# The last pass of a SwiGLU down projection: one bank at a time, and two kinds of additions on GpSimd

## The chip, the cores and the metric

One core of a Trainium2 chip. The metric is the device time of one execution in microseconds (us), lower is better. The kernel's output is compared with a float32 reference. Engines are named as in the profile: PE (TensorE, with its weight loads PEld), DVE (VectorE), ACT (ScalarE), POOL (GpSimd) and SP (SyncE, which here only issues DMAs).

## The reference

One decoder layer on 512 tokens of width 2048: a mixer of 16 attention heads with an output projection and a residual, then a SwiGLU block with a residual. All of it is float32. The change lies in the SwiGLU block, in its last product:

```python
def _swiglu(h, w_gate, w_up, w_down):
    return (jax.nn.silu(h @ w_gate) * (h @ w_up)) @ w_down

# D_MODEL = 2048, SEQ = 512, D_FF = 5632
x = x + _hybrid_mixer(_rms_norm(x, attn_norm[l]), ...)
h = _rms_norm(x, ffn_norm[l])
x = x + _swiglu(h, w_gate[l], w_up[l], w_down[l])
```

## The kernel before

**Arithmetic.** Every float32 operand of a matmul is split into a high part and the rest ("split": ACT copies the operand into the rounded format, DVE subtracts the copy from the operand). A product is then three matmuls: high by high, high by rest, rest by high. In the code `w[0]`, `w[1]` are the two parts of a weight, `a[0]`, `a[1]` those of the activations. All DVE work of two operands goes through the helper `tt` (L77), all ACT copies through `act` (L80), so these two lines stand for many steps, and the tiles' names tell them apart.

**Block products.** The gate, up and down products are cut into 2 by 2 blocks, and the blocks are multiplied by schemes that need seven products in place of eight, with sums of weights and of activations made beforehand and sums of results made afterwards. Time up to about 1684 us is the mixer and the gate and up products; the change does not touch them.

**Down product.** It runs from about 1684 us to 2120 us, in four passes (`ps_` = 0 to 3, here pass 1 to pass 4). Passes 1 and 2 make one half of the output rows, passes 3 and 4 the other. The first pass of each pair (1 and 3) does four of the seven products, the second (2 and 4, `second` true in the code) does the other three. A pass goes over 22 steps j of the inner dimension; a step with its matmuls is called a *block* here, counted from 0. Output columns of the weight are in four *quarters* q of 128, each with its own two banks of PSUM, `b[q][0]` and `b[q][1]`. A block of a second pass is 4 quarters x 3 products x 3 matmuls = 36 matmuls of 256 columns. The three products are listed in `DOWN2` (activation part, weight part, bank, half of the bank): the first goes to bank 1, the other two fill the two halves of bank 0.

**What comes before a block.** `got(j)` fetches ahead (`load_a`, `load_w`, DMAs issued by SP) and calls `splits(i)`. In a second pass `splits` first makes the sum of the freshly loaded weight `r[:, :T]` and a sum `t` that was kept from the pass before (`keep_t2`; in the profile `wd<-wd,t2m` or `wd<-wd,rawm`, 512 columns). This is "the sum with kept halves". Then come three splits, each a copy by ACT and a difference by DVE: the activations (768 columns, `rawm`), the kept sum `t` (512, `t2m` or `rawm`), and the pair of `r` (1024, `wd`), which needs the sum. The last block of pass 4 splits its activations last. The split weights lie in four places in turn (`WAT`), the split activations in three (`AAT`), the raw weights in three (`RING`). A block's activations can thus be copied when PE has finished the block three before it.

**Order.** From the end of the mixer on, the instructions of DVE, ACT, POOL and SP are pinned: each of these engines issues in the order in which the code makes them (`pin`, `fetch2`). The matmuls are not pinned; the compiler may move them among each other. Each of the engines waits only in its own queue.

**The last blocks of a pass** (one block, in pass 4 three together: `tail`) run quarter by quarter, and behind each quarter its results are taken from PSUM by `end(q)`, which is `last(q)`:

- passes 1 and 3: `keep1` puts the two banks into the kept tiles `cb` and `ca`. Behind pass 3, `fold_early` is left to be done during pass 4, one step per block (`next(pending, None)` after `got`): for each quarter a difference of 512 columns, one of 256, then twice a product with `rstd` on DVE and an accumulating DMA from `x1d` issued by POOL (L1019). These are 16 steps, in blocks 0 to 15 of pass 4. They are called the *fold*.
- pass 2: `finish_late`, whose rest is done during pass 3.
- pass 4: `finish(q)`: t4 = bank 1 x rstd; `ca` - t4 (the stored difference), which leaves as `out[n + 1]`; half of `cb` + t4; t62 = bank 0 x rstd; `cb` + t62, which leaves as `out[n]`. DVE does all five, SP issues the two DMAs. In the profile both t4 and t62 are `t<-pd,rstd`.

Of the kernel before, what the change touches and what calls it, by code (L numbers as in the profile page):

```python
# [12 lines left out]
OP = mybir.AluOpType  # L13
# [4 lines left out]
P = 128  # L18
D = 2048
T = 512  # L20
# [6 lines left out]
NJ = NF // 2  # L27
# [41 lines left out]
def hybrid_layer(ctx: ExitStack, tc: tile.TileContext, xT, vec, ffb, wfg, wfirst, win, cmpw, wout, wgu, wdn, out):  # L69
    nc = tc.nc  # L70
    pinned = [False]

    def pin(ins):
        return tc.keep_in_program_order(ins) if pinned[0] else ins

    def tt(*args, op):
        return pin(nc.vector.tensor_tensor(*args, op=op))  # L77
# [21 lines left out]
    def big(i):  # L99
        at = i * 2 * T + OFF_BIG[i]  # L100
        return bigm[:, at:at + 2 * T].rearrange("p (s t) -> p s t", s=2)
# [23 lines left out]
    def ftile(name):  # L125
        return pers.tile([P, T], F32, tag="f", name=name, bufs=4)
# [12 lines left out]
    def load_w(src, name):  # L139
        n = src.shape[-1]  # L140
        st = wpl.tile([P, HALF * P], F32, tag="ws", name=f"ws_{name}", bufs=3)
        load(st[:, :n], src)
        wp = wpl.tile([P, 2, HALF * P], FR, tag="wp", name=f"wp_{name}", bufs=2)
        split(wp[:, :, :n], st[:, :n])
        return wp
# [22 lines left out]
    def run(steps):  # L168
        for _ in steps:
            pass  # L170
# [86 lines left out]
    for g in range(2):  # L257
        t = ap_.tile([P, NB, 64], F32, name=f"pc{g}")
# [21 lines left out]
    live = {}  # L280
# [275 lines left out]
    def chain(*gens):  # L556
        for g in gens:
            yield from g
# [12 lines left out]
    for k in range(NK):  # L571
        xs = oxp.tile([P, T], F32, tag="ox", name=f"x_{k}", bufs=16)
        nc.sync.dma_start(xs, xT[k])
        ws = oxp.tile([P, T], F32, tag="ox", name=f"w0_{k}", bufs=16)
        nc.sync.dma_start(ws, wfirst[k])
        t = big(k)
# [13 lines left out]
        for hl in range(2):  # L590
            nc.tensor.matmul(first[4][:64], wf[:, k], t[:, hl], start=(k == 0 and hl == 0),
                             stop=(k == NK - 1 and hl == 1))
# [48 lines left out]
    h = NH - 1  # L641
# [18 lines left out]
    for i, h in enumerate(order[:-1]):  # L660
        t = big(i)
# [3 lines left out]
    t = big(NK - 1)  # L665
# [10 lines left out]
    def cut(m, at, n):  # L676
        return m[:, at:at + n]
# [117 lines left out]
    def halves(x):  # L795
        return x.rearrange("p (h t) -> p h t", h=2)

    def both(x):
        return x[:, None].to_broadcast([P, 2, 256])
# [55 lines left out]
    def fetch2(dst, src):  # L855
        d = nc.sync.dma_start(dst, src)
        tc.keep_in_program_order(d)
        return d

    def t2(j):  # L860

        m, at = (live["fa"], j - 8) if 8 <= j < 16 else (live["fy"], j if j < 8 else j - 8)
        return cut(m, at * T, T)

    def pass_of(i):
        return i // (2 * NJ), i // NJ % 2, i % NJ
# [20 lines left out]
    def load_a(i):  # L887
        second, j = pass_of(i)[1:]
        at = (8 + 2 * (turn[1] % 3)) * T
        turn[1] += 1  # L890
        rawa[i] = cut(live["fa"], at, (3 if second else 4) * 256)
        d = fetch2(rawa[i], ad[j][:, 4:7] if second else ad[j][:, 0:4])
        if i == 2:
            tc.add_manual_dep(d.ins, live["w0"].ins.name, PACE)

    def split2(dst, src):
        h = act(dst[0], src, AF.Copy)
        tt(dst[1], src, dst[0].bitcast(F32), op=OP.subtract)
        return h

    def keep_t2(i):
        r = raww.pop(i)
        tt(t2(i % NJ), r[:, T:2 * T], r[:, 2 * T:3 * T], op=OP.add)

    def splits(i):
        second, j = pass_of(i)[1:]
        n = 3 if second else 4
        m, at = WAT[i % 4]
        w = [cut(m, at + h * (4 * T + (SHIFT if i % 24 == 0 else 0)), n * T) for h in range(2)]
        m, at = AAT[i % 3]  # L910
        a = [cut(m, at + h * 4 * 256, n * 256) for h in range(2)]
        if second:
            r, t = raww.pop(i), t2(j)
            tt(r[:, T:2 * T], r[:, :T], t, op=OP.add)
        if i < 4 * NJ - 1:
            split2(a, rawa.pop(i))
        if second:
            split2([x[:, 2 * T:] for x in w], t)
            split2([x[:, :2 * T] for x in w], r[:, :2 * T])
        else:  # L920
            live.setdefault("w0", split2(w, raww[i]))
        if i == 4 * NJ - 1:
            split2(a, rawa.pop(i))
        return [[x.rearrange("p (f c) -> p f c", f=n) for x in y] for y in (w, a)]
# [19 lines left out]
    for j in range(NJ):  # L944
        for which in range(2):
            q = [ps.tile([P, T], F32, tag=tag, name=f"q{which}{j}_{i}", bufs=BUFS[tag])
                 for i, tag in enumerate(SETS[which])]
            for g in range(NG):
# [14 lines left out]
                w = split_w.pop(i)  # L963

                for wp in range(2):
                    for kk in range(2):
                        k = 2 * (ORDER[i] % NG) + kk
                        a = forms[k]
                        cs = slice(kk * P, (kk + 1) * P)
                        for fa, fb, b, h in PROD:  # L970
                            o = q[b][:, h * 256:(h + 1) * 256]
                            for xp in range(2 - wp):
                                nc.tensor.matmul(o, w[wp][:, fb, cs], a[:, xp, fa],  # L973
                                                 start=(k == 0 and h == 0 and wp == 0 and xp == 0),
                                                 stop=(g == NG - 1 and kk == 1 and wp == 1), skip_group_check=True)
# [24 lines left out]
    def banks(name, tags):  # L1000
        return [ps.tile([P, T], F32, tag=tag, name=f"{name}_{i}", bufs=BUFS[tag]) for i, tag in enumerate(tags)]
# [51 lines left out]
    def finish(q, b):  # L1053

        y = [k[:, q] for k in kept]
        n = 8 + 2 * q
        t4, t62 = ftile(f"t4_{q}"), ftile(f"t62_{q}")
        tt(halves(t4), both(b[1][:, :256]), halves(rstd), op=OP.mult)
        tt(y[1], y[1], t4, op=OP.subtract)
        fetch2(out[n + 1], y[1])  # L1060
        tt(y[0][:, :256], y[0][:, :256], t4[:, :256], op=OP.add)
        tt(t62, b[0], rstd, op=OP.mult)
        tt(y[0], y[0], t62, op=OP.add)
        fetch2(out[n], y[0])

    TAGS = ("ss", "to", "gg", "mt")
    for ps_ in range(4):
        p, second = ps_ // 2, ps_ % 2
        b = [banks(f"pd{ps_}{i}", t) for i, t in enumerate(TAGS)]
        prods = DOWN2 if second else DOWN1  # L1070
        ends = []
        extra = chain(load_w(2 * NJ), load_w(2 * NJ + 1)) if ps_ == 1 else iter(())

        def got(j):
            i = ps_ * NJ + j
            if i not in ahead:
                load_a(i)
                run(load_w(i))
                ahead[i] = splits(i)
                if not second:  # L1080
                    keep_t2(i)
            return j, *ahead.pop(i)

        def block(js, parts, end=None):
            ws = [got(j) for j in js]
            if end and ps_ < 3:

                run(extra)
                nxt = [(ps_ + 1) * NJ + n for n in range(2)]
                for i in nxt:  # L1090
                    load_a(i)
                    run(load_w(i) if i not in raww else ())
                for i in nxt:
                    ahead[i] = splits(i)
                    if ps_ == 1:
                        keep_t2(i)
            if ps_ == 0 and js[0] == 0:
                for _ in range(3):
                    next(pending)
                for i in range(2):  # L1100
                    keep_t2(i)
            next(pending, None)
            for qs in parts:
                for j, w, a in ws:
                    for q in qs:
                        for fa, fb, k, h in prods:
                            for xp in range(2):
                                nc.tensor.matmul(b[q][k][:, h * 256:(h + 1) * 256], w[0][:, fb, q * P:(q + 1) * P], a[xp][:, fa],  # L1108
                                                 start=(j == 0 and h == 0 and xp == 0), stop=False, skip_group_check=True)
                for q in qs:  # L1110
                    for fa, fb, k, h in prods:
                        for j, w, a in ws:
                            nc.tensor.matmul(b[q][k][:, h * 256:(h + 1) * 256], w[1][:, fb, q * P:(q + 1) * P], a[0][:, fa],  # L1113
                                             start=False, stop=(j == NJ - 1), skip_group_check=True)
                    if end:
                        end(q)

        def last(q):
            if not second:
                keep1(q, b[q])  # L1120
                if p:
                    ends.append(fold_early(q))
            elif p:
                finish(q, b[q])
            else:
                ends.append(finish_late(q, b[q]))
                next(ends[-1])

        each = [(q,) for q in range(4)]
        head, tail = 2 if ps_ == 0 else 1, 3 if ps_ == 3 else 1  # L1130
        block(tuple(range(head)), [range(2), range(2, 4)] if ps_ == 0 else each)
        for j in range(head, NJ - tail):
            block((j,), [range(4)])
            if j >= 16:
                next(extra, None)
        run(pending)
        block(tuple(range(NJ - tail, NJ)), each, last)
        pending = chain(*ends)

# [69 lines left out]
```

## Time and profile before

| | |
|---|---|
| median of 3 runs | 2127.51 us (2127.18 to 2128.12) |
| the profiled execution | 2128.19 us, its span 2126.4 us |
| PE | 2114.6 us busy (99%) |
| DVE | 1693.4 us busy (80%) |
| ACT | 995.5 us busy (47%) |
| POOL | 185.2 us busy (9%) |
| DMA | 349.56 MB, mean 164 GB/s |

The span is the time from the first to the last instruction that the profile has; the time of the execution contains some 1.8 us more around it. Times in the rows of a timeline are microseconds from the start of the span; a row has start, duration, engine, line, operation, the tiles written and read, the shape, the count of merged instructions and in brackets the idle time before it with what ended it. A row that merges several instructions shows their start and their whole stretch. Ends of matmuls are modelled.

### The profile page before, as it was taken

To read this page: it belongs to the slowest core of one execution; us is meant where nothing else is said; L and a number is where in the kernel's file an instruction comes from. 1 tells how busy PE (TensorE), PEld (TensorE's weight loads), DVE (VectorE), ACT (ScalarE), POOL (GpSimd) and SP (SyncE) were. 2 spreads that over 40 slices of the span, in tenths; PEclk is the share of its full clock that TensorE was granted. 3 is DMA by queue.
4 is the path that set the end of the run, shared out by engine and by line. 5 is a ranking of instruction groups with operands and counts; after the bars stand their busy time and mean duration, and the time that the engine had idled before them with its cause. 6 is when DMAs were issued, how large, how long until landed. Compare 5 with 4: busy or idle time off the path is not lost.

```text
span 2126.4 us, 36981 instructions
## 1 busy us (share of the span) xinstructions
PE 2114.6 (99%) x15137; PEld 1957.9 (92%) x15137; DVE 1693.4 (80%) x2488; ACT 995.5 (47%) x1226; POOL 185.2 (9%) x283
## 2 busy tenths in 40 slices
PE   9999999999999999999999999999999999999998
PEld 7888887888888888999999999999999999999998
DVE  6678568555657444999999999999999987889998
ACT  5455455444446333544334444343443455565553
POOL 0000000111101000111111111111111000000000
PEclk9999999999999999999999999999999999999999
DMA  5421211222222443567776777777777798479864
GB/s 194 158 73 35 67 60 45 83 86 87 87 85 65 158 143 125 162 194 211 183 198 187 185 202 187 198 190 183 205 185 199 226 337 266 150 235 330 291 180 138
DMA packets 113482, 349.56 MB, mean 164 GB/s; under 512 B 13592, under 2 KB 13592, under 8 KB 113312
## 3 DMA queue, kind: packets, MB, share of 16 engines
q1 hardware_dynamic: 85552, 270.33, 38.5%
q0 software_dynamic: 22144, 52.44, 13.6%
q10 hardware_dynamic: 5616, 24.43, 2.9%
q8 instruction: 118, 1.93, 0.4%
q14 instruction: 52, 0.43, 0.1%
HBM read 318.56 MB, written 74.73 MB: 185 GB/s over the span
## 4 chain that ended last, share of the span: by engine, by line
PE 95%; DVE 3%; ACT 1%; issue 0%; DMA 0%; ACTq 0%; DVEq 0%
PE q L973 39%; PE pd L1108 13%; PE pd L1113 6%; PE po L150 2%; PE po L148 2%; PE po L149 2%; PE ps_kf L148 1%; PE ps_kf L150 1%; PE ps_kf L149 1%; PE ps_qf L148 1%; PE ps_vf L148 1%; PE ps_qf L150 1%; PE ps_qf L149 1%; PE ps_vf L150 1%; PE ps_vf L149 1%; PE ps_qn L149 1%
## 5 line engine op out<-in xcount | busy, mean ns | idle before, releaser
L80 ACT ACTIVATE bigm<-r 128x1792 fp32r<-128x1792 f32 x174 | 298.1, 1713 | 463.0 <-PE q L973 267.7
L77 DVE TENSOR_TENSOR bigm<-r,bigm 128x1792 fp32r<-128x1792 f32 x174 | 351.5, 2020 | 14.2 <-ACT bigm L80 13.4
L77 DVE TENSOR_TENSOR r<-r 128x512 f32<-128x512 f32 x522 | 267.2, 512 | 26.3 <-DMA r<-wgu 14.2
L973 PE MATMUL q<-bigm 128*128 128x256 f32 x1848 | 217.5, 277 | 0.3
L973 PE MATMUL q<-forma,bigm 128*128 128x256 f32 x1848 | 217.0, 277 | 0.0
L973 PE MATMUL q<-formx,bigm 128*128 128x256 f32 x1848 | 217.0, 277 | 0.0
L973 PE MATMUL q<-formy,bigm 128*128 128x256 f32 x1848 | 216.8, 277 | 0.0
L973 PEld LDWEIGHTS q<-bigm 128*128 128x128 f32 x1848 | 213.2, 188 | 0.7 <-ACT bigm L80 0.3
L973 PEld LDWEIGHTS q<-forma,bigm 128*128 128x128 f32 x1848 | 213.2, 188 | 0.1
L973 PEld LDWEIGHTS q<-formx,bigm 128*128 128x128 f32 x1848 | 213.1, 188 | 0.0
L973 PEld LDWEIGHTS q<-formy,bigm 128*128 128x128 f32 x1848 | 212.9, 188 | 0.1
L122 POOL DMA_DIRECT2D wsum<-wdn x176 | 119.8, 687 | 881.2 <-ACT bigm L80 776.9
L1108 PE MATMUL pd<-bigm 128*128 128x256 f32 x1224 | 148.0, 277 | 0.0
L1108 PEld LDWEIGHTS pd<-bigm 128*128 128x128 f32 x1224 | 143.1, 188 | 0.0
L77 DVE TENSOR_TENSOR bigm<-wd,bigm 128x2048 fp32r<-128x2048 f32 (+1 forms) x64 | 110.3, 1723 | 12.0 <-ACT bigm L80 11.8
L80 ACT ACTIVATE bigm<-rawm 128x768 fp32r<-128x768 f32 (+2 forms) x72 | 65.9, 925 | 108.6 <-PE pd L1113 63.5
L148 PE MATMUL po<-bigm,wp_o 128*128 128x512 f32 x256 | 100.0, 391 | 0.7 <-ACT wp_o L80 0.5
L150 PE MATMUL po<-bigm,wp_o 128*128 128x512 f32 x256 | 99.7, 390 | 0.2 <-DVE wp_o L77 0.2
L149 PE MATMUL po<-bigm,wp_o 128*128 128x512 f32 x256 | 99.7, 390 | 0.0
L77 DVE TENSOR_TENSOR bigm<-rawm,bigm 128x768 fp32r<-128x768 f32 (+2 forms) x72 | 75.4, 1056 | 26.7 <-ACT bigm L80 26.1
L80 ACT ACTIVATE bigm<-wd 128x2048 fp32r<-128x2048 f32 (+1 forms) x64 | 93.2, 1456 | 5.7 <-DVE wd L77 2.5
L1113 PE MATMUL pd<-bigm 128*128 128x256 f32 x612 | 81.3, 277 | 0.0
(487 smaller groups left out, 4075.0 us busy)
## 6 DMA issues: line engine op xcount, KB each, us to landing
r<-wgu SPq DMA_DIRECT2D x174, 512.0 KB, 4.3
wsum<-wdn POOLq DMA_DIRECT2D x176, 256.0 KB, 4.8
rawm<-ad SPq DMA_DIRECT2D x44, 512.0 KB, 6.6
wd<-wdn SPq DMA_DIRECT2D x40, 512.0 KB, 5.8
wd<-wsum SPq DMA_DIRECT2D x40, 512.0 KB, 6.9
ad<-cb ACTq DMA_DIRECT2D x22, 896.0 KB, 5.4
rawm<-ad SPq DMA_DIRECT2D x44, 384.0 KB, 3.5
ws_o<-wout SPq DMA_DIRECT2D x28, 512.0 KB, 3.6
```

Of the source, the lines that this page charges most:

```text
L77: return pin(nc.vector.tensor_tensor(*args, op=op))
L80: return pin(nc.scalar.activation(*args, **kw))
L122: d = nc.gpsimd.dma_start(step[0], step[1], **step[2])
L148: nc.tensor.matmul(o, lh, rh, start=start, stop=False)
L149: nc.tensor.matmul(o, lh, rl, start=False, stop=False)
L150: nc.tensor.matmul(o, ll, rh, start=False, stop=stop)
L973: nc.tensor.matmul(o, w[wp][:, fb, cs], a[:, xp, fa], start=(k == 0 and h == 0 and wp == 0 and xp == 0), stop=(g == NG - 1 and kk == 1 and ...
L1108: nc.tensor.matmul(b[q][k][:, h * 256:(h + 1) * 256], w[0][:, fb, q * P:(q + 1) * P], a[xp][:, fa], start=(j == 0 and h == 0 and xp == 0), ...
L1113: nc.tensor.matmul(b[q][k][:, h * 256:(h + 1) * 256], w[1][:, fb, q * P:(q + 1) * P], a[0][:, fa], start=False, stop=(j == NJ - 1), skip_g ...
```

## The change

Three things.

1. In `splits`, the sum with kept halves (second passes, 44 in all) is made by POOL instead of DVE. It stands at the same place of the code and is pinned, so it takes its place in POOL's queue.
2. In the last three blocks of pass 4, each quarter's matmuls go product group by product group: first the one product of bank 1 for all three blocks (9 matmuls), then the two products of bank 0 (18 matmuls). `end(q)` is called after each group.
3. `finish` becomes a generator of two parts: after bank 1 come t4, the stored difference, its output and the half addition; after bank 0 come t62, its addition and the last output. The stored difference is made by POOL instead of DVE.

```diff
@@ splits
         if second:
             r, t = raww.pop(i), t2(j)
-            tt(r[:, T:2 * T], r[:, :T], t, op=OP.add)
+            pin(nc.gpsimd.tensor_tensor(r[:, T:2 * T], r[:, :T], t, op=OP.add))
@@ finish
         tt(halves(t4), both(b[1][:, :256]), halves(rstd), op=OP.mult)
-        tt(y[1], y[1], t4, op=OP.subtract)
+        pin(nc.gpsimd.tensor_tensor(y[1], y[1], t4, op=OP.subtract))
         fetch2(out[n + 1], y[1])
         tt(y[0][:, :256], y[0][:, :256], t4[:, :256], op=OP.add)
+        yield
         tt(t62, b[0], rstd, op=OP.mult)
         tt(y[0], y[0], t62, op=OP.add)
         fetch2(out[n], y[0])
+        yield
@@ block
             for qs in parts:
-                for j, w, a in ws:
+                for some in ((prods[:1], prods[1:]) if end and ps_ == 3 else (prods,)):
+                    for j, w, a in ws:
+                        for q in qs:
+                            for fa, fb, k, h in some:
+                                for xp in range(2):
+                                    nc.tensor.matmul(... w[0] by a[xp] ...)
                     for q in qs:
-                        for fa, fb, k, h in prods:
-                            for xp in range(2):
-                                nc.tensor.matmul(... w[0] by a[xp] ...)
-                for q in qs:
-                    for fa, fb, k, h in prods:
-                        for j, w, a in ws:
-                            nc.tensor.matmul(... w[1] by a[0] ...)
-                    if end:
-                        end(q)
+                        for fa, fb, k, h in some:
+                            for j, w, a in ws:
+                                nc.tensor.matmul(... w[1] by a[0] ...)
+                        if end:
+                            end(q)
@@ last
             elif p:
-                finish(q, b[q])
+                next(live.setdefault(f"end{q}", finish(q, b[q])))
```

More of the change, by code (lines that the diff above doesn't have):

```diff
@@ L1103, in block @@
             for qs in parts:
-                for j, w, a in ws:
-                    for q in qs:
-                        for fa, fb, k, h in prods:
-                            for xp in range(2):
-                                nc.tensor.matmul(b[q][k][:, h * 256:(h + 1) * 256], w[0][:, fb, q * P:(q + 1) * P], a[xp][:, fa],
-                                                 start=(j == 0 and h == 0 and xp == 0), stop=False, skip_group_check=True)
-                for q in qs:
-                    for fa, fb, k, h in prods:
-                        for j, w, a in ws:
-                            nc.tensor.matmul(b[q][k][:, h * 256:(h + 1) * 256], w[1][:, fb, q * P:(q + 1) * P], a[0][:, fa],
-                                             start=False, stop=(j == NJ - 1), skip_group_check=True)
-                    if end:
-                        end(q)
+                for some in ((prods[:1], prods[1:]) if end and ps_ == 3 else (prods,)):
[3 more added lines that the diff above has]
+                                for xp in range(2):
+                                    nc.tensor.matmul(b[q][k][:, h * 256:(h + 1) * 256], w[0][:, fb, q * P:(q + 1) * P], a[xp][:, fa],
+                                                     start=(j == 0 and h == 0 and xp == 0), stop=False, skip_group_check=True)
+                    for q in qs:
+                        for fa, fb, k, h in some:
+                            for j, w, a in ws:
+                                nc.tensor.matmul(b[q][k][:, h * 256:(h + 1) * 256], w[1][:, fb, q * P:(q + 1) * P], a[0][:, fa],
+                                                 start=False, stop=(j == NJ - 1), skip_group_check=True)
+                        if end:
+                            end(q)
         def last(q):
```

## The prediction

> **What bounds the kernel now.** I read the page first, then who TensorE waits for, then busy time by stage, then the order of work in the last passes.
>
> ```profile
> span 2126.4 us, 36981 instructions
> PE 2114.6 (99%) x15137; PEld 1957.9 (92%) x15137; DVE 1693.4 (80%) x2488; ACT 995.5 (47%) x1226; POOL 185.2 (9%) x283
> PE pd L1108 <- ACT formx L80: 0.4, 1, 0.4
> 1815.00:1895.00 80.00, 80.00 (x707) 80.00 (x707) 66.03 (x82) 47.18 (x62) 0.00 (x0) 1.00 0.56 182
> 2040.00:2100.00 60.00, 60.00 (x531) 60.00 (x530) 55.57 (x73) 34.72 (x46) 5.12 (x6) 1.00 0.70 197
> ```
>
> TensorE (PE) is busy throughout; from 2000 us on it waits once, for 0.4 us. The last two lines (columns: stretch, PE, weight loads, DVE, ACT, POOL, clock, DMA) are the inside of the two second passes, the passes whose split the change touches. In the first of them VectorE (DVE) is 83% busy, in the last 93%: there it also makes the fold, the leftover work of pass 3. So a gain can only come from the end, where DVE works after PE has stopped, and from that one wait; a loss can come only if the split of the last pass can no longer keep ahead of PE.
>
> **The end.** The change lets t4 (made from bank 1) start before bank 0 is filled.
>
> ```profile
> 2119.50 0.28 PE L1113 MATMUL pd<-formx,bigm 128*128 128x256 f32 x1
> 2119.97 0.68 DVE L77 TENSOR_TENSOR t<-pd,rstd 128x512 f32<-128x512 f32 x1
> 2120.69 0.69 DVE L77 TENSOR_TENSOR ca<-ca,t 128x512 f32<-128x512 f32 x1
> 2121.30 0.42 DVE L77 TENSOR_TENSOR cb<-cb,t 128x256 f32<-128x256 f32 x1
> 2121.63 0.69 DVE L77 TENSOR_TENSOR t<-pd,rstd 128x512 f32<-128x512 f32 x1
> 2122.35 0.69 DVE L77 TENSOR_TENSOR cb<-cb,t 128x512 f32<-128x512 f32 x1
> 2123.07 0.33 SPq L856 DMA_DIRECT2D out<-cb  x1
> ```
>
> Columns: start, duration, engine and line, instruction. After the last matmul DVE makes five steps, then the last output leaves; from its issue to the end of the span are 3.3 us, which stay. In the new order bank 1 is done 18 matmuls ahead of the end, t4 and the half addition fall beside those, and t62 starts at 2119.97 instead of 2121.63: 1.66 us less. The difference goes to GpSimd (POOL); its output leaves before the last one. If it holds up the half addition, some tenths go back, so I take **-1.6**. Per quarter DVE then has four steps, 0.7 + 0.33 + 0.7 + 0.7 = 2.4 us, where five took 3.1 (2119.97 to 2123.07), so it falls behind PE no more than now.
>
> **The moved sums.** 44 sums of 512 columns, 0.61 us each from start to start, go from DVE to POOL. No two-input POOL instruction is in this trace. The nearest rows:
>
> ```profile
> 344.16 0.69 POOL L543 TENSOR_SCALAR nbf<-ckb,ncq 128x512 f32<-128x512 f32 x1 [24.64 <-issue]
> 344.46 1.47 DVE L77 TENSOR_TENSOR wp_qf<-ws_qf,wp_qf 128x1024 fp32r<-128x1024 f32 x1 [0.46 <-ACT wp_qf L80]
> 344.92 1.15 POOL L544 TENSOR_SCALAR_AFFINE_SELECT nbf<-nbf 128x128 f32<-128x128 f32 x1
> 395.49 1.23 DVE L77 TENSOR_TENSOR wp_qf<-ws_qf,wp_qf 128x1024 fp32r<-128x1024 f32 x1
> 411.37 0.37 POOL L543 TENSOR_SCALAR nbf<-ckb,ncq 128x128 f32<-128x128 f32 x1 [1.38 <-DVE st_f L331]
> 411.81 0.29 POOL L544 TENSOR_SCALAR_AFFINE_SELECT nbf<-nbf 128x128 f32<-128x128 f32 x1
> 414.46 1.73 POOL L543 TENSOR_SCALAR nbf<-ckb,ncq 128x512 f32<-128x512 f32 x1 [2.36 <-DVE st_f L331]
> 414.48 1.24 DVE L77 TENSOR_TENSOR wp_kf<-ws_kf,wp_kf 128x1024 fp32r<-128x1024 f32 x1
> ```
>
> One input of 512 columns costs 0.69 us, of 128 columns 0.37: 0.42 us for the stream of 512, 0.27 fixed. If the second input is streamed after the first, the sum costs **S = 0.27 + 2 x 0.42 = 1.12 us**; I take that, between 0.69 (both at once) and 1.73 (the longest row, which stood behind DVE). The rows also show a collision: at 344.46 DVE takes 1.47 us instead of 1.23 while POOL is still in its work, then POOL's small select takes 1.15 us instead of 0.29 and ends just after DVE. So each holds the other off, less some 0.15 us of start-up. [...]
>
> **Where the sums stand.** A block of the last pass:
>
> ```profile
> 2034.04 0.69 DVE L77 TENSOR_TENSOR cb<-cb,rstd 128x512 f32<-128x512 f32 x1
> 2061.55 0.85 ACT L80 ACTIVATE bigm<-rawm 128x768 fp32r<-128x768 f32 x1 [1.76 <-issue]
> 2062.43 0.96 DVE L77 TENSOR_TENSOR bigm<-rawm,bigm 128x768 fp32r<-128x768 f32 x1 [0.45 <-ACT bigm L80]
> 2062.82 1.05 ACT L80 ACTIVATE formx<-wd 128x1024 fp32r<-128x1024 f32 x1
> 2063.31 0.68 DVE L77 TENSOR_TENSOR formx<-rawm,formx 128x512 fp32r<-128x512 f32 x1
> 2063.91 1.22 DVE L77 TENSOR_TENSOR formx<-wd,formx 128x1024 fp32r<-128x1024 f32 x1
> 2065.04 0.68 DVE L77 TENSOR_TENSOR cb<-cb,rstd 128x512 f32<-128x512 f32 x1
> 2065.63 1.37 ACT L80 ACTIVATE bigm<-rawm 128x768 fp32r<-128x768 f32 x2 [1.76 <-issue]
> 2065.65 0.69 DVE L77 TENSOR_TENSOR wd<-wd,rawm 128x512 f32<-128x512 f32 x1
> 2066.02 0.85 POOL L1019 DMA_DIRECT2D cb<-x1d  x1 [11.36 <-DVE cb L77]
> ```
>
> ACT copies the activations (2061.55, again at 2065.63, 4.08 later: PE's pace, 36 matmuls of 0.113), DVE makes three differences (0.88 + 0.60 + 1.13 = 2.61 from start to start), the fold's product with rstd (0.61), and the sum for the next block (2065.65).
>
> In pass 2 there is no fold: DVE has 3.22 us in each 4.08. It loses the 0.61 and is held S - 0.15 = 0.97: 3.58 us, still under 4.08, so **0**. (Were S 1.73, it would be 4.19: 0.11 over in each of 20 blocks, 2.2 us. A split starts when PE has two blocks before it, 8.2 us, and takes 3.6, from 2061.55 to the end of its last difference at 2065.13: the lead of 4.6 absorbs that.)
>
> **The last pass** differs, because POOL's queue there also holds the fold's accumulating DMAs. One starts 0.30 us after its product (2065.72, 2066.02). Now the next block's sum is in POOL's queue, behind this DMA, which waits for the product, which DVE makes after this block's last difference. So a loop closes that is open today: from a product's end 0.30, DMA 0.85, 0.07 to the next POOL instruction (344.85, 344.92), sum 1.12, 0.07 to ACT taken like the hop before, ACT's copy of the pair 1.05, 0.04 (2063.87, 2063.91), the difference 1.13, next product 0.68: **5.31 us**, against PE's 4.08. In each quarter of the fold (four blocks) two blocks have a product with a DMA; the other two pass without one, 2.61 + 0.33 and 2.61 + 0.61. Sum 10.62 + 2.94 + 3.22 = 16.8 us; one more of the four sums falls on busy DVE, + 0.97 = **17.8**, against 16.3 for PE.
>
> The fold takes one step per block from block 0 on, so products stand in blocks 2 and 3, 6 and 7, 10 and 11, 14 and 15. The first one ends at 2034.73 today, 0.61 earlier without the sum ahead of it, 2034.12. Three quarters later, in block 14: 2087.4; the last product, block 15: 2092.7; the difference of block 16: 2097.4; blocks 17 to 20 at 2.61 + 0.97: 2111.7; block 21's three differences (2.7): the last ends at **2114.4**. What that displaces:
>
> ```profile
> 2105.85 0.68 DVE L77 TENSOR_TENSOR wd<-wd,t2m 128x512 f32<-128x512 f32 x1
> 2106.18 1.86 PE L1108 MATMUL pd<-bigm 128*128 128x256 f32 x15
> 2106.61 1.06 ACT L80 ACTIVATE bigm<-wd 128x1024 fp32r<-128x1024 f32 x1 [1.43 <-issue]
> 2107.58 0.83 ACT L80 ACTIVATE formx<-rawm 128x768 fp32r<-128x768 f32 x1
> 2108.46 0.50 PE L1108 MATMUL pd<-formx,bigm 128*128 128x256 f32 x2 [0.41 <-ACT formx L80]
> 2108.85 0.95 DVE L77 TENSOR_TENSOR formx<-rawm,formx 128x768 fp32r<-128x768 f32 x1
> 2109.86 0.74 PE L1108 MATMUL pd<-formx,bigm 128*128 128x256 f32 x4
> ```
>
> Today that difference ends at 2109.80, and the matmuls that need it start at once (2109.86). 2114.4 - 2109.8 = **+4.6**: PE's end moves by as much, in waits spread over the later blocks, since the copies of a late sum reach PE late too. Sum: + 4.6 - 1.6 = **+3.0 us**. The profiled execution took 2128.19 us (span 2126.4), the median of the runs is 2127.51: I add to the median, **2130.5**. Each 0.1 us of S counts fifteen times (three per quarter, six after): 1.5 us. The 0.2% that a measurement of this kernel can tell is 4.25 us, and S = 1.20 reaches it.
>
> **Rivals.**
> (A) *The cover holds.* If collisions cost DVE nothing, or S is near 0.69, a quarter takes 16.8 or less, the lead of the copies is not used up, and the last difference is ready at about 2108. Then the sum of block 21 no longer waits behind DVE (2105.85) and ACT's two copies come earlier: the wait at 2108.46 goes too (15 matmuls at 0.113 end at 2107.88, so 0.6). -1.6 - 0.6: **2125.3**. For it: ACT has slack, and PE's wait shows that the sum's place matters. Against: the rows at 344 and 414.
> (B) The forecast, 2130.5; with S from 1.0 to 1.3, 2128.7 to 2133.2.
> (C) *DVE keeps the port.* Nothing shows who goes first when DVE has its next instruction ready as POOL waits. If DVE always does, a sum that meets it starts only when DVE runs dry: 1.12 + 0.07 + 1.05 + 0.04 = 2.3 us in place of 0.97, + 1.3 in each quarter and in every second of the later blocks, + 6.5: **2137.0**. It decides as soon as DVE is never idle, which 93% in the last pass nearly is.
> (D) *The order is not as written.* The 15 matmuls at 2106.18 are more than the 12 that the first quarter has from these two blocks, so the compiler mixes quarters. If it fills bank 0 first, the 1.6 us stay: 2132.1.
>
> **How the numbers follow.** A 0.33, B 0.45, C 0.17, D 0.05. S = 1.20 is the middle of 0.69 and 1.73, so B is slower by over 0.2% with 0.25 and within it with 0.20. Slower: 0.25 + 0.17 + 0.02 = 0.44. Faster by over 0.2% would need 4.25 us, twice what A has: 0.02 of A's share. The rest, 0.54, is within. The range goes from just under A to C's value, 2124.8 to 2137.2; half of C and an S over 1.55 lie outside.
>
> **What would show it.** S is the duration of POOL's new instruction where DVE is idle. The end is right if t62's product starts 0.2 us after the last matmul. The loop is right if two products with rstd in neighbouring blocks stand over 5 us apart (4.1 today), and PE's waits in the last pass name ACT's copies and DVE's differences. If PE has no wait there, A holds; if POOL's sums begin only in DVE's gaps, C. Waits of PE in pass 2, or a change before 1800 us, would mean that I looked in the wrong place.

## The result: 2141.8 us, slower

The changed kernel takes 2141.84 us (median of 4 runs, 2140.39 to 2142.22), the kernel before 2127.61 us (median of 4, 2127.18 to 2128.12): ratio 1.0065, 95% interval 1.0052 to 1.0077. That is 14.2 us slower, above the range 2124.8 to 2137.2. The profiled execution took 2141.84 us.

The first two lines of the profile page of the changed kernel, and then the waits of PE from the start of the down product to the end (columns: who waited for whom; us in total, times, longest):

```profile
span 2140.0 us, 37077 instructions
PE 2119.3 (99%) x15137; PEld 1959.4 (92%) x15137; DVE 1695.8 (79%) x2440; ACT 994.1 (46%) x1226; POOL 260.8 (12%) x331
PE pd L1112 <- ACT bigm L80: 3.9, 5, 1.1
PE pd L1112 <- DVE formx L77: 1.8, 1, 1.8
PE pd L1112 <- DVE bigm L77: 1.6, 1, 1.6
PE pd L1117 <- DVE bigm L77: 0.4, 2, 0.2
PE pd L1112 <- ACT formx L80: 0.3, 1, 0.3
```

One wait of 0.4 us has become ten of 8.0 us, for ACT's copies and DVE's differences, the names that the prediction gave for its loop. PE's share on the page is 99% in both kernels, so this share alone would hide the whole loss.

By stage, from the start of the first to the start of the last matmul of each pass (pass 1 begins at 1699.0 us in the kernel before): passes 1 and 3 are unchanged (119.8 and 119.7 us), pass 2 takes 90.17 us (89.74 before), **pass 4 takes 103.61 us (90.94 before)**. From the start of the last matmul to the end of the span, here called the *tail*, are 7.87 us (6.87). So 12.7 us are lost in pass 4, 1.0 in the tail, 0.4 in pass 2, together 14.1. (The 0.4 does not come from moving the sums as such: sums_defer and sums_nodma below have the same 22 sums of pass 2 on POOL and take 89.74.)

Busy time in stretches of pass 4 (columns as in the prediction: stretch, PE with its matmuls, weight loads, DVE, ACT, POOL, granted clock, DMA), the first line from the kernel before, the others from the changed one:

```profile
2060.00:2106.00 46.00, 46.00 (x408) 46.00 (x408) 41.11 (x53) 26.06 (x34) 3.41 (x4) 1.00 0.58 167
...
2060.00:2106.00 46.00, 41.77 (x345) 40.12 (x345) 41.45 (x37) 24.45 (x32) 18.01 (x16) 1.00 0.61 161
2106.00:2120.20 14.20, 10.25 (x83) 9.44 (x81) 11.90 (x13) 6.16 (x9) 7.33 (x3) 1.00 0.31 95
2121.50:2124.90 3.40, 3.40 (x19) 3.40 (x18) 3.21 (x6) 0.00 (x0) 1.90 (x2) 0.52 0.21 81
```

Where 408 matmuls ran, 345 run: 63 x 0.113 = 7.1 us go while the fold is made. In the last blocks before DVE's last difference, 83 run where 14.2 / 0.113 = 125 fit: 4.8 us. And from 2121.5 to 2124.9 PE never waits, but its clock is granted at 0.52, and matmuls start 0.21 us apart instead of 0.113: about 1.6 us. (The three come to 13.5, more than 12.7, because they are counted against a steady 0.113. The kernel before has lost some 1.2 us against that too: its 791 steps from matmul to matmul in pass 4 would take 89.7 us, and it takes 90.94.)

**The loop.** A quarter of the fold in the timeline of the changed kernel:

```profile
2039.17 0.69 DVE L77 TENSOR_TENSOR ca<-ca,rstd 128x512 f32<-128x512 f32 x1
2040.37 0.89 POOL L1019 DMA_DIRECT2D ca<-x1d  x1 [3.48 <-issue]
2040.64 5.00 DVE L77 TENSOR_TENSOR bigm<-t2m,bigm 128x512 fp32r<-128x512 f32 x1
2041.00 4.08 POOL L914 TENSOR_TENSOR wd<-wd,t2m 128x512 f32<-128x512 f32 x3
2045.56 1.21 DVE L77 TENSOR_TENSOR bigm<-wd,bigm 128x1024 fp32r<-128x1024 f32 x1
2046.70 0.68 DVE L77 TENSOR_TENSOR ca<-ca,cb 128x512 f32<-128x512 f32 x1
2052.85 0.68 DVE L77 TENSOR_TENSOR cb<-cb,rstd 128x512 f32<-128x512 f32 x1
2053.82 0.87 POOL L1019 DMA_DIRECT2D cb<-x1d  x1 [8.74 <-DVE cb L77]
2054.43 1.71 POOL L914 TENSOR_TENSOR wd<-wd,t2m 128x512 f32<-128x512 f32 x1
2056.18 1.06 ACT L80 ACTIVATE bigm<-wd 128x1024 fp32r<-128x1024 f32 x1 [5.65 <-POOL wd L914]
2057.27 1.23 DVE L77 TENSOR_TENSOR bigm<-wd,bigm 128x1024 fp32r<-128x1024 f32 x1 [2.27 <-ACT bigm L80]
2058.41 0.69 DVE L77 TENSOR_TENSOR ca<-ca,rstd 128x512 f32<-128x512 f32 x1
```

From 2052.85 on, the chain runs as forecast: product, DMA, sum, copy (it waited "<-POOL wd"), difference ("<-ACT bigm"), next product at 2058.41, 5.56 us later. POOL's second DMA (2040.37) is followed by something not forecast: three sums that had heaped up behind it run back to back, 4.08 us, and DVE's step of 2040.64, which takes 0.69 us elsewhere, takes 5.00 and ends at 2045.64, 0.56 us after the run. POOL keeps DVE out through the whole run.

**The end.** The last two steps of DVE, its output and POOL's last difference, then the closing instructions (a view by line: duration in ns min/median/max, first to last start), first of the changed kernel and then of the one before:

```profile
2131.52 1.51 POOL L1059 TENSOR_TENSOR ca<-ca,t 128x512 f32<-128x512 f32 x1 [1.52 <-DVE t L77]
2132.17 0.28 PE L1117 MATMUL pd<-formx,bigm 128*128 128x256 f32 x1
2132.48 0.69 DVE L77 TENSOR_TENSOR t<-pd,rstd 128x512 f32<-128x512 f32 x1 [0.58 <-PE pd L1117]
2133.21 0.69 DVE L77 TENSOR_TENSOR cb<-cb,t 128x512 f32<-128x512 f32 x1
2133.93 0.33 SPq L856 DMA_DIRECT2D out<-cb  x1
L1208 POOLq DRAIN  x3: 46/102/7767, 2131.5 to 2139.8; - x3
L1208 SPq DRAIN  x3: 7/7/7, 2136.4 to 2139.5; - x3
...
L1204 POOLq DRAIN  x3: 46/93/8235, 2086.4 to 2126.1; - x3
```

The last output leaves 1.76 us after the last matmul starts, before it was 3.57 (2119.50 to 2123.07): 1.8 us gained, as forecast. But POOL's closing drain (the instruction that closes an engine's program here), issued at 2131.5, lasts 7.77 us, to 2139.3, 6.2 us beyond POOL's last difference, and the span ends behind it. SP was through at 2136.4. In the kernel before, the drain took 8.2 us too, from 2086.4, hidden under PE.

### The profile page after: what moved, and what is told of

Read it like the earlier page. It is cut to its first block, busy times and chain, and to the rows that moved or that the text cites. A ratio compares the mean times of both kernels' runs of the same rounds, so it can differ in the third digit from the quotient of the medians.

```text
span 2140.0 us, 37077 instructions
## 1 busy us (share of the span) xinstructions
PE 2119.3 (99%) x15137; PEld 1959.4 (92%) x15137; DVE 1695.8 (79%) x2440; ACT 994.1 (46%) x1226; POOL 260.8 (12%) x331
## 5 line engine op out<-in xcount | busy, mean ns | idle before, releaser
L77 DVE TENSOR_TENSOR bigm<-r,bigm 128x1792 fp32r<-128x1792 f32 x174 | 351.5, 2020 | 14.9 <-ACT bigm L80 14.1
L1112 PE MATMUL pd<-bigm 128*128 128x256 f32 x1224 | 151.4, 278 | 4.2 <-ACT bigm L80 2.4
L77 DVE TENSOR_TENSOR bigm<-rawm,bigm 128x768 fp32r<-128x768 f32 (+2 forms) x72 | 88.9, 1243 | 26.2 <-ACT bigm L80 25.6
L1117 PE MATMUL pd<-bigm 128*128 128x256 f32 x612 | 82.2, 277 | 0.4 <-DVE bigm L77 0.4
```

## Experiments

My theory: the eight sums right behind an accumulating DMA of the fold cost pass 4 its time (the loop), and the end loses its gain to POOL's drain. Rivals: every moved sum costs some by shutting DVE out, wherever it stands (the "port theory" of the expectations; the runs show that the two engines shut each other out, but not whether a port is the cause); or the new order of the matmuls costs it. Each comparison is with the kernel before on the same chip, whose median was 2127.9 to 2128.0 there. For pass 4 (90.94 us before) and tail (6.87) the profiled executions are compared.

| kernel | median us | ratio (95%) | pass 4 | tail |
|---|---|---|---|---|
| end_pool | 2129.78 | 1.0008 (0.9999 to 1.0017) | 90.94 | 8.69 |
| end_dve | 2127.85 | 0.9998 (0.9989 to 1.0007) | 90.58 | 6.84 |
| sums_only | 2140.48 | 1.0058 (1.0046 to 1.0071) | 103.40 | 6.03 |
| sums_pass2 | 2128.04 | 1.0001 (0.9992 to 1.0010) | 90.58 | 7.17 |
| sums_defer | 2136.11 | 1.0035 (1.0021 to 1.0049) | 97.12 | 6.00 |
| sums_nodma | 2130.17 | 1.0010 (1.0001 to 1.0020) | 93.79 | 6.02 |
| sums_behind | 2136.49 | 1.0040 (1.0025 to 1.0056) | 99.28 | 7.18 |
| sums_others | 2127.26 | 0.9997 (0.9988 to 1.0006) | 91.40 | 6.00 |
| diff_q012 | 2127.17 | 0.9993 (0.9985 to 1.0002) | 90.58 | 6.31 |
| diff_q012_last | 2126.16 | 0.9992 (0.9983 to 1.0001) | 90.57 | 5.29 |
| best_last3 | 2126.03 | 0.9992 (0.9983 to 1.0000) | 90.33 | 5.28 |

### The halves apart

**end_pool**: the changed kernel with the sums back on DVE; the new order and the stored difference on POOL remain.

```diff
-            pin(nc.gpsimd.tensor_tensor(r[:, T:2 * T], r[:, :T], t, op=OP.add))
+            tt(r[:, T:2 * T], r[:, :T], t, op=OP.add)
```

> The changed end (bank 1 first, finish in two parts, stored difference on POOL), all 44 sums back on DVE. Two theories of the end. Drain theory: in the changed kernel SP is done with the outputs 4.3 us after the start of the last matmul (6.1 before), but POOL joins the closing barrier only 7.1 us after it, 6 us behind its own last instruction, the stored difference; so the outputs leave 1.8 us earlier and the execution still ends 1.0 later: 2128.6 us against 2127.6, with no wait of PE beyond the one of 0.4 us. Rival, the prediction's own step: the end gains 1.6 us, and the late barrier comes from the sums: 2126.0 us.

**end_dve**: the stored difference on DVE as well; only the order and the two parts of `finish` remain.

```diff
-        pin(nc.gpsimd.tensor_tensor(y[1], y[1], t4, op=OP.subtract))
+        tt(y[1], y[1], t4, op=OP.subtract)
```

> The same end, but the stored difference is made by DVE too, so that POOL has nothing to do after the fold. Drain theory: POOL is at the barrier long before SP, and what the end saves is seen in full: 1.6 to 1.8 us, 2125.8 to 2126.0. Rival (the barrier is late for another reason, such as the two-part end itself): as end_pool, about 2128.6.

**sums_only**: the kernel before with all 44 sums on POOL. **sums_pass2**: only pass 2's 22 sums.

```diff
-            tt(r[:, T:2 * T], r[:, :T], t, op=OP.add)
+            pin(nc.gpsimd.tensor_tensor(r[:, T:2 * T], r[:, :T], t, op=OP.add))
```

> The kernel before with all 44 sums on POOL and nothing else. Both theories of the sums (queue behind the fold's DMAs; port collisions as such) expect pass 4 longer by the 12.7 us that the changed kernel shows, and an end as before: 2140.3. If the new order of banks has a part in the waits of the last three blocks, it is less, about 2138.

> The kernel before with the 22 sums of pass 2 on POOL, those of pass 4 on DVE. Queue theory (the loss is the sums' place behind the fold's DMAs, which pass 2 has not): within 0.5 us of before, 2127.1 to 2128.1. Rival (each sum on POOL costs because it keeps DVE from the port): half of the 44 sums, half of the loss, about + 6 us, 2133.6.

The sums alone cost pass 4 12.5 us; neither the order nor the stored difference costs it anything, so that rival is out. Pass 2's sums, on the same two engines but with no DMA on POOL's queue, cost nothing that can be measured. But DVE has only 3.22 us of work in each 4.08 there, so there is room for a collision, and pass 2 alone does not tell the place in the queue from the load of DVE. The four kernels of the next section do.

The end was a surprise twice. In end_pool PE ends as before and the tail is 1.8 us longer, where 1.0 was expected. Its closing instructions:

```profile
L1208 POOLq DRAIN  x3: 46/93/7749, 2119.7 to 2128.0; - x3
L1208 SPq DRAIN  x3: 7/7/7, 2124.4 to 2127.7; - x3
```

SP is through at 2124.4, before it was 2125.5, so the outputs did leave earlier; the drain of 7.75 us from 2119.7 then decides. And end_dve, which has no drain to wait for, gains nothing, where 1.6 to 1.8 were expected. Its steps of DVE in the last quarter, with t4 of the first:

```profile
2109.93 0.69 DVE L77 TENSOR_TENSOR t<-pd,rstd 128x512 f32<-128x512 f32 x1 [0.82 <-PE pd L1117]
...
2118.91 0.68 DVE L77 TENSOR_TENSOR t<-pd,rstd 128x512 f32<-128x512 f32 x1
...
2120.58 0.68 DVE L77 TENSOR_TENSOR t<-pd,rstd 128x512 f32<-128x512 f32 x1
2121.29 0.69 DVE L77 TENSOR_TENSOR cb<-cb,t 128x512 f32<-128x512 f32 x1
```

From the first t4 to the fourth are 8.98 us, 2.99 for each quarter, with no gap, against 3.06 for a quarter's 27 matmuls. DVE starts late (the bank 1 of quarter 0 is full only after the last split; the first row shows DVE idle for 0.82 us, waiting for PE) and catches up by only 0.07 us a quarter, so t62 starts at 2120.58 although bank 0 was filled before. When PE is late instead, as in the changed kernel, DVE has time and the full 1.8 us show.

### What in the sums costs the time

**sums_defer**: sums_only, and each accumulating DMA is issued one block later, so that the next block's sum stands ahead of it. **sums_nodma**: sums_only without the eight DMAs, which leaves the residual out of half of the output.

```diff
-            pin(nc.gpsimd.dma_start(y[i], x1d[8 + 2 * q + i], accum_op=OP.add))
             yield
+            pin(nc.gpsimd.dma_start(y[i], x1d[8 + 2 * q + i], accum_op=OP.add))   # sums_defer only
```

> All 44 sums on POOL, nothing else of the change; but each accumulating DMA of the fold is issued one block later, behind the next block's sum instead of ahead of it. The work of every engine is the same. Queue theory (the sum waits behind a DMA that waits for DVE, and sums heaped up behind it then keep DVE from the port in one run): the loop is open, pass 4 within 2 us of the kernel before, 2126.5 to 2129.5. Port theory (44 collisions cost, wherever the sums stand in the queue): as sums_only, 2140.

> All 44 sums on POOL, nothing else of the change; the fold's eight accumulating DMAs are left out (so the residual is missing from half of the output), its DVE work stays. Queue theory: POOL never waits for DVE in pass 4 and makes each sum when its weights land, no runs of three, pass 4 within 2 us of before: 2126.5 to 2129.5. Port theory: DVE has 2.61 + 0.97 to 1.1 of being kept out + about 0.5 of the fold in each block, 4.2 us against 4.08 in fourteen blocks, and as many collisions as in sums_only: 2135 to 2140.

Without the DMAs pass 4 loses 2.9 us, not 12.5 (0.5 of it by the sums, the rest below). With the DMAs a block later the profiled execution loses 6.2 in pass 4; it was the fastest of the four, and the median is 8.1 us above the kernel before. Both forecasts for sums_defer missed. Its trace shows the loop open, and beside it what the sums cost DVE by shutting it out. A quarter of the fold there (columns as above), and rows from it:

```profile
2068.44:2086.37 17.93, 17.93 (x161) 17.93 (x160) 17.93 (x17) 10.11 (x13) 7.70 (x6) 1.00 0.70 177
...
2074.69 2.25 DVE L77 TENSOR_TENSOR bigm<-rawm,bigm 128x512 fp32r<-128x512 f32 x1
2074.80 3.30 POOL L914 TENSOR_TENSOR wd<-wd,rawm 128x512 f32<-128x512 f32 x2
2076.86 2.32 DVE L77 TENSOR_TENSOR bigm<-wd,bigm 128x1024 fp32r<-128x1024 f32 x1
```

DVE is never idle in this quarter, so nothing in it waits for a sum. But its own steps come to 12.6 us (4 x 2.61 + 2 x 0.61 + 0.33 + 0.61). The other 5.3 are four steps in which a sum shuts it out, by 1.1 to 1.6 us each, as in the two rows (0.69 and 1.22 elsewhere). That makes 17.9 against PE's 16.3. In sums_nodma it is 1.1 for each of the four, 17.0 a quarter. In the changed kernel a quarter is 12.6 + 4.0 (the run of three) + 2.3 (the wait for the fourth sum, as at 2057.27) = 18.9, and 19.0 in the trace. So a sum that meets DVE as a rule takes more from it than the 0.61 that it spares, wherever it stands in the queue; the loop comes on top.

**sums_behind**: the kernel before with POOL making only the eight sums right behind a DMA (blocks 3, 4, 7, 8, 11, 12, 15, 16 of pass 4). **sums_others**: only the other 14 of pass 4.

```diff
+            if i - 3 * NJ in (3, 4, 7, 8, 11, 12, 15, 16):   # sums_others: i >= 3 * NJ and ... not in
+                pin(nc.gpsimd.tensor_tensor(r[:, T:2 * T], r[:, :T], t, op=OP.add))
+            else:
+                tt(r[:, T:2 * T], r[:, :T], t, op=OP.add)
```

> Only eight sums on POOL, those of pass 4 that stand in its queue right behind one of the fold's DMAs (blocks 3, 4, 7, 8, 11, 12, 15, 16); the other 36 on DVE. So no sum follows another on POOL, and DVE is never shut out for a run. Loop theory (a product, its DMA, the next block's sum, ACT's copy, the difference, the next product: 5.57 us in the changed kernel): a quarter takes 2 x 5.57 + 2.94 + 3.22 + 2 x 0.61 for DVE's own sums = 18.5 us against 16.3, which ends the last difference 6 to 7 us later: 2133 to 2135. Run theory (the loss is that sums heaped up on POOL keep DVE out for 4 us): within 1 us of before, 2127 to 2129.

> The complement within pass 4: its other fourteen sums on POOL, the eight behind a DMA and all of pass 2 on DVE. Loop theory: no sum that is needed next waits for DVE; a quarter takes 2 x (2.61 + 0.61 + 0.61) + 2.94 + 3.22 + 2 x 1.09 for two collisions = 16.0 us against 16.3, so nothing is lost, and the last block's wait is 0.6 shorter: 2127.0 to 2128.0. Run theory: two sums still run one behind the other after the second DMA of a quarter, and DVE is out for 2.5 us there: 2130 or more. Port theory: fourteen collisions, 2131.

The eight cost pass 4 8.3 us (the median, 2136.49, is 1.5 above the loop theory's range, about what the slowed clock costs that is described below), the 14 others 0.5, and their median is no different from the kernel before. In sums_behind the loop has the larger part: DVE waits 2.9 us of a quarter and is shut out for 1.6. Products in neighbouring blocks there, and the same place a quarter later,

```profile
2052.51 0.69 DVE L77 TENSOR_TENSOR cb<-cb,rstd 128x512 f32<-128x512 f32 x1
2058.07 0.69 DVE L77 TENSOR_TENSOR ca<-ca,rstd 128x512 f32<-128x512 f32 x1
...
2070.85 0.69 DVE L77 TENSOR_TENSOR cb<-cb,rstd 128x512 f32<-128x512 f32 x1
```

stand 5.56 us apart, and the quarter takes 18.3 us against PE's 16.3. Eight and 14 together would cost 8.8, not 12.5. The rest comes only when both kinds are on POOL: then sums heap up behind the DMA, as the row of 5.00 us showed, and the last blocks come later still. The changed kernel waits 1.6 and 1.8 us for DVE there, sums_behind once:

```profile
PE pd L1111 <- ACT formx L80: 2.6, 1, 2.6
```

### The clock

A term I had not thought of stands in the same traces. A stretch of the last blocks, first of sums_nodma, then of sums_others:

```profile
2111.60:2114.80 3.20, 3.20 (x17) 3.20 (x16) 2.41 (x5) 0.00 (x0) 0.00 (x0) 0.51 0.21 82
...
2111.60:2114.80 3.20, 3.20 (x29) 3.20 (x29) 3.13 (x6) 0.00 (x0) 0.00 (x0) 1.00 0.42 164
```

and the rows of PE and DVE around the wait in sums_nodma, and the wait of PE in sums_others:

```profile
2108.87 0.94 DVE L77 TENSOR_TENSOR formx<-rawm,formx 128x768 fp32r<-128x768 f32 x1
2109.87 0.74 PE L1107 MATMUL pd<-formx,bigm 128*128 128x256 f32 x4 [2.12 <-DVE formx L77]
2111.65 2.12 PE L1107 MATMUL pd<-bigm 128*128 128x256 f32 x9
...
PE pd L1111 <- DVE formx L77: 1.0, 1, 1.0
```

After a wait of 2.1 us the granted clock falls to 0.51 in this stretch, and 17 matmuls run where 29 did; after one of 1.0 us it stays at 1.00. The same slow stretch stands in all five kernels that lost over 2 us (the changed one, sums_only, sums_defer, sums_nodma, sums_behind), with a wait of 1.8 to 2.6 us each; it is 3.41 us long in the changed kernel (2121.62 to 2125.03 below) and, estimated from the clock and the matmuls of their stretches, about as long in the others. The length of one wait is not all: in the changed kernel a wait of 1.6 us that ended at 2115.89 left the clock at 1.00. Four stretches of that kernel, the first three of 3.41 us:

```profile
2114.79:2118.20 3.41, 1.98 (x14) 1.77 (x14) 3.41 (x5) 2.24 (x4) 0.22 (x1) 1.00 0.00 0
2118.20:2121.61 3.41, 1.59 (x14) 1.39 (x14) 2.58 (x3) 0.00 (x0) 0.00 (x0) 1.00 0.02 5
2121.62:2125.03 3.41, 3.41 (x19) 3.41 (x18) 3.09 (x6) 0.00 (x0) 2.03 (x2) 0.50 0.25 98
2125.04:2132.00 6.96, 6.96 (x63) 6.96 (x63) 4.82 (x8) 0.00 (x0) 3.02 (x3) 1.00 0.40 155
```

With PE busy for 1.98 of 3.41 us the clock stayed, with 1.59 it fell. In the other four kernels PE was busy for 1.0 to 1.4 of the 3.41 us before the fall.

And sums_nodma shows more: its last difference ends at 2109.81, the kernel before has it at 2109.80. Counted from the start of pass 4, which is 0.5 us earlier there, that is 0.5 us later; so the lead of the split absorbs most of what the 22 sums cost DVE. PE waits because the compiler put the nine matmuls of 2111.65, which don't need that difference, behind those that do; in the kernel before they run ahead of them. The same nine stand behind in all seven kernels that make the last block's sum on POOL, and ahead in the other six. So their place is an effect of the moved sum too, through the compiler. In sums_others it costs 0.5 us, although the last difference comes 0.6 us *earlier* in its pass than in the kernel before. The 2.9 us of sums_nodma are the 0.5, nine matmuls, 1.0, and 1.4 more, which the slow clock can account for (16 matmuls 0.21 us apart instead of 0.113: 1.6).

### The end, mended

**diff_q012**: end_pool with the last quarter's stored difference back on DVE, so that POOL ends a quarter earlier. **diff_q012_last**: the last block's sum on POOL in addition. **best_last3**: the sums of the last three blocks on POOL.

```diff
+        if q < 3:
             pin(nc.gpsimd.tensor_tensor(y[1], y[1], t4, op=OP.subtract))
+        else:
+            tt(y[1], y[1], t4, op=OP.subtract)
```

> end_pool, but the last quarter's stored difference is made by DVE, the other three by POOL; sums on DVE. Drain theory (POOL joins the closing barrier 6 us behind its last work): POOL's last work now ends some 2.8 us earlier, the barrier is no longer late, and the end shows the 1.3 us by which end_pool's last output left earlier, less up to 0.3 for the added step: 2126.7 to 2127.3 against 2128.0. Rival (the barrier is late because POOL has worked at all in the last stretch, or because of DVE's port): as end_pool, 2129.8.

> diff_q012 with one sum moved to POOL, that of the very last block. Backlog theory (end_dve and end_pool: DVE is busy without a gap from the first t4 on, so the end is set by when quarter 0's bank 1 is full, and that by PE's wait for the last split, which stands behind this sum on DVE): PE's wait of 0.6 us goes, the first t4 starts more than 1 us earlier, and the end is PE's last matmul + 0.2 + two DVE steps: 2125.2 to 2126.0. Rival (the end is bound by DVE's five steps per quarter): as diff_q012.

> diff_q012 with the sums of the last three blocks on POOL instead of the last one alone (bank 1 first, three of four stored differences on POOL). In diff_q012_last DVE's sum of block 20 took 1.78 us, because POOL's sum of block 21 held it up, and PE still waits 0.8 us for the last splits. If both sums are on POOL ahead of time, these waits go: 2125.3 to 2125.8 against 2126.2 for diff_q012_last and 2128.0 for before. Rival (three sums on POOL run one behind the other and keep DVE out as in the changed kernel): 2126.2 to 2127.5.

With POOL's last work a quarter earlier, its drain ends only 0.2 us behind SP (2124.44 and 2124.27; in end_pool 2127.47 and 2124.43), and the tail falls from 8.69 to 6.31 us. With the last sum off DVE, t4 of the first quarter starts earlier,

```profile
2109.41 0.69 DVE L77 TENSOR_TENSOR t<-pd,rstd 128x512 f32<-128x512 f32 x1 [0.83 <-PE pd L1123]
```

1.0 us earlier in its pass than in diff_q012 (81.0 us from the pass's start, 82.1 there). DVE no longer drags its backlog to the end: the last t62 starts 0.4 us after the last matmul's start (1.4 in diff_q012), and the tail is 5.29. That is the 1.6 us of the prediction, had in full, but only with two further changes, and about half of it comes without the new end: the four kernels with the old end and the last block's sum on POOL have tails of 6.0 us (6.9 to 7.2 with that sum on DVE). best_last3 is 1.9 us below the kernel before and some 15.8 below the changed one. Its median is the lowest, but diff_q012_last has the same ratio, so nothing tells the two apart, and both stand 0.2 us above what was expected of them. And 0.08% is less than the 0.2% that a measurement can tell from nothing; the interval ends at 1.0000.

## Why the prediction was wrong

The direction was right, and so was half of the mechanism (the loop through POOL's queue, in pass 4 only); the size was not: 3.0 us forecast, 14.2 measured. The step that failed is the count of the sums that shut DVE out. By its steps:

- **Pass 2, 0**: held (+ 0.4 in the trace, nothing in sums_pass2's time).
- **S**: forecast 1.12 us; the sums in a run start 1.25 us apart, and one alone takes 1.3. Inside the loop, from the start of the DMA to the end of the sum, 2054.43 + 1.71 - 2053.82 = 2.32 us against 0.85 + 0.07 + 1.12 = 2.04. So the loop is 5.56 us, not 5.31: 0.25 each time.
- **The quarter, 17.8 us; here the main step failed.** From 2033.44 to 2052.85 are 19.4, the later ones 19.0. In the first: 5.73 to the next product, then 7.53 to the fold's next step (2039.17 to 2046.70) where 5.31 + 0.97 were taken, then 6.15 as forecast (2.94 + 3.22). I had let two of a quarter's four sums be waited for (2 x 2.09, the 5.31 less 3.22) and one more collide with DVE, for 0.97. In fact one is waited for (2.3), and the three that the second DMA holds back come out in a run that shuts DVE out for 4.0, 1.35 for each. I had listed what is queued behind the DMA, but only the first of it, and had put a collision at 0.97 where 1.1 to 1.6 were measured. Three quarters and the last loop: + 4.4 (the fold's last product ends at 2097.05, forecast 2092.7).
- **Blocks 16 to 21**: the last difference ends at 2120.17, forecast 2114.4. Beside the 4.4, + 1.4: one more run of three in block 16 (a step of 4.74 us; the block's difference ends 6.65 us after the last product, forecast 4.7), less 0.5 in the five blocks behind it. In block 19 the opposite of a run that DVE waits for: a sum that DVE held until it ran dry, with a wait of 2.27 us for its copy. That is rival C's mechanism, in one place.
- **PE's end moves as the last difference does**: that moved 10.4 us, PE 12.7. Of the other 2.3, the slow clock is 1.6 and nine matmuls that stood ahead of that difference and now stand behind it are 1.0 (17 of the last three blocks' 108 are done when it comes, 26 before). Some 0.4 goes back: in the kernel before the last matmuls start 0.118 us apart, here 0.113.
- **The end, - 1.6**: the outputs left 1.8 us earlier, but the tail is 1.0 longer; the drain was missing from the sum. And "it falls behind PE no more than now" holds only where PE is late: in end_dve the backlog ate the gain.

Together: the 3.0 forecast, + 4.4 (quarters), + 1.4 (blocks 16 to 21), + 2.3 (PE behind the difference), + 2.6 (the end), + 0.4 (pass 2) = 14.1 us. Rival A is refuted by the ten waits, D by t62's start 0.31 us behind the last matmul's. The range failed because S alone was allowed to vary, while the number of sums that meet DVE was given one value and one rival, and the clock, the matmuls' order and the drain were put at nothing.

## What to carry to other kernels

An instruction moved to an idle engine inherits that engine's queue (here the sum stood behind a DMA that waits for DVE, and two products came to be 5.56 us apart). Look for the entry in it that waits for the engine you want to relieve, and count everything that will stand behind that entry, not only the first. Then ask what the moved work takes from the relieved engine if the two shut each other out: here a sum spares DVE 0.61 us and shuts it out for 1.1 or more; in pass 2, where DVE has room (3.22 us of work in each 4.08), that cost nothing that can be measured. A move that is harmless by itself (14 sums, 0.5 us) can add half again to the harm of another (8 sums, 8.3 us; together 12.5). And before the last work of a program goes to another engine, see in the trace how long that engine's closing drain is (POOL's took 7.7 to 8.5 us here), and whether something still covers it.

## What the runs showed of the hardware

- **GpSimd and VectorE shut each other out.** A single sum of POOL that met DVE as a rule kept it out for 1.1 us in sums_nodma, for 1.1 to 1.6 in sums_defer. In the changed kernel three back to back turned one 0.69-us step of DVE into 5.00 us: DVE did not get in between them. The other way round, in the changed kernel:

```profile
2107.69 7.33 POOL L914 TENSOR_TENSOR wd<-wd,t2m 128x512 f32<-128x512 f32 x3 [5.67 <-DMA wd<-wdn]
2107.71 1.21 DVE L77 TENSOR_TENSOR formx<-wd,formx 128x1024 fp32r<-128x1024 f32 x1
2112.66 1.23 DVE L77 TENSOR_TENSOR bigm<-wd,bigm 128x1024 fp32r<-128x1024 f32 x1 [2.27 <-ACT bigm L80]
```

Three sums take 7.33 us, not 4.1: the first waits until DVE, busy since before 2107.7, runs dry at 2110.4, and its copy and difference come that much later (2112.66). But a run is not always closed: DVE's step of 2112.66 takes its usual 1.23 us while POOL's third sum waits, and in sums_defer DVE's step of 2074.69 ends at 2076.94, inside POOL's pair (2074.80 to 2078.10). What decides whether the other engine gets in stays open.
- **Behind waits of about 2 us the granted clock fell to half.** PE's waits of 1.8 to 2.6 us came with a stretch at a granted clock of 0.50 to 0.51, in five kernels (3.41 us long in the changed one, by estimate about as long in the others); shorter ones, up to 1.6 us, left it at 1.00. In the 3.41 us before the clock fell PE was busy for 1.0 to 1.6 us; with 1.98 it did not fall. Where the boundary lies between these cases the runs do not show.
- **POOL's closing drain** takes 7.7 to 8.5 us from its issue, wherever it stands: 8.2 from 2086.4 in the kernel before, 8.5 from 2085.7 in end_dve, 7.8 from 2116.7 in diff_q012, 7.7 from 2119.7 in end_pool, 7.8 from 2131.5 in the changed kernel. In the last two it ends 6.2 us behind POOL's last work and decides the end: that work is over 7.0 us before the span is (2133.0 of 2140.0, 2121.3 of 2128.3). In the kernel before the drain is over at 2094.6 of 2126.4 and does not show.
